# The delta stage's written order: masks ahead of the key scaling, value copies ahead of the exponentials, decayed products behind the state updates

## The chip, the cores and the metric

The kernel runs on one core of one Trainium2 chip. The metric is the device time of one execution in microseconds (us), the median of several runs. Five engines work side by side, each through its own queue in order: PE (TensorE, the matmuls, with its weight loads listed apart as PEld), DVE (VectorE), ACT (ScalarE), POOL (GpSimd) and SP (SyncE, which issues most of the DMAs here). An engine whose next instruction waits on a semaphore holds everything that stands behind it.

## What is computed

Two layers of a bidirectional hybrid encoder over 2048 tokens of width 1024. Each layer normalises its input, projects it, and runs two branches: a gated delta rule with four heads, scanned forward and backward in chunks, and a convolution module. Both are projected, merged with sigmoid gates, projected once more and added to the input. The stage that matters here is the chunked delta rule (the kernel uses chunks of 128 tokens):

```python
lmat = jnp.where(strict, jnp.einsum('bhncd,bhnsd->bhncs', k_beta, k) * decay, 0.0)
sol = lax.linalg.triangular_solve(eye + lmat, rhs, left_side=True, lower=True, unit_diagonal=True)
attn = jnp.einsum('bhncd,bhnsd->bhncs', q, k) * decay
...
def step(state, inp):
    val_n, kc_n, a_n, qd_n, kd_n, dl_n = inp
    v_new = val_n - jnp.einsum('bhcd,bhde->bhce', kc_n, state)
    o_n = jnp.einsum('bhcd,bhde->bhce', qd_n, state) + jnp.einsum('bhcs,bhse->bhce', a_n, v_new)
    state = state * dl_n[..., None, None] + jnp.einsum('bhcd,bhce->bhde', kd_n, v_new)
    return state, o_n
```

Each step needs the state of the step before: this is a chain that no reordering shortens. `decay` is the exponential of differences of cumulated log decays, masked to one triangle; it does not depend on the state, so it can be prepared ahead.

## The kernel before

Each layer runs a projection stage (dense matmuls, convolutions, per-head preparation), then `delta()`, then `merge()`. A dense matmul of float32 values is made of three passes (L173 to L175) over split operands: weights `whi`/`wlo` and inputs `hi`/`lo`. `weight()` (L159) loads a block by DMA into `wraw`, then ACT copies `whi` and DVE subtracts to give `wlo`.

`delta()` (L816) runs 16 steps; at each one the forward direction takes chunk `step` and the backward direction chunk `15 - step` (two lanes). Three kinds of work are written into one another:

- **The scan**, `lane()` (L956), in three parts. Part A: PE multiplies keys and queries with the state (L968, L971), DVE updates the values (L973), ACT copies the query part scaled into `o1` (L977), and in steps 8 to 15, where the other direction's output of this chunk is already stored, POOL adds it (`old`, L979). Part B: PE applies the inverse (L983), ACT copies the new values `vn` out of PSUM (L985). Part C: PE forms the state update and the output (L992, L1001), DVE updates the state (L995) and adds the output (L1003 or L1008).
- **The preparation** of later steps, `prep()` (L866): loads (`gb` from `gc_d`, `k` and `g` from `g_d`, inverse blocks); masks on POOL (L889) and exponentials on ACT (L892) of `gb`; transposes, copies (L896 to L904) and the products with the decay (L906, L908) on DVE; then four groups of small matmuls that assemble the inverse `wt` (L915; L925 and L928 with the copies L930 to L934; L939 and L940 with L942; L948 and L949 with L950 and L951). It is a generator; `go(i)` runs the next part for step `i`. The ring of `gb` has two buffers, one preparation's worth, so the `gc_d` loads of the next preparation wait for L908 of this one.
- **`finish()`** (L1014) of a step's two outputs from step 8 on: squares, the reciprocal root of their means, scaling, transposes, store.

`decay_keys` (L854) scales the next step's keys on POOL. Between these parts `pull(n)` takes `n` steps of dense work from a filler, one step being three matmul passes of 512 columns. The filler runs the second half of the gate projection, `gates(1)`: 16 column blocks times 2 times 8, or 256 steps. Then `early_merge()` (L1124, called from `filler()`, L1118) loads `u` by four DMAs, splits it in four pieces, and gives 64 more steps. A `yield GAP` ends a pull at once, without dense work: one stands behind the four loads of `u`, one behind each split.

`bind()` (L87) fixes the order of PE, ACT, DVE and POOL inside `delta()` to the order in which the program writes it. SP is not fixed: a planner orders its DMAs by its own estimate of when they are ready. `LEAD` gives the pulls before step 0, `STEP` the four pulls of a step, 17 dense steps in all.

The order of one step before: part A, inverse part 1 of step+1, key scaling, masks and exponentials of step+2, reciprocal root, pull 5; part B, output scaling, products of step+2, inverse part 2 of step+1, pull 4; part C, inverse part 3, loads of step+3, squares, pull 4; transposes, inverse part 4, pull 4.

Of the kernel before, what the change touches and what calls it, by code (L numbers as in the profile page):

```python
# [10 lines left out]
ALU = mybir.AluOpType  # L11
# [14 lines left out]
R1 = 3.0  # L26
R3 = 4.5
GAP = 0
LEAD = (16, 6, 8, 6, 4)
STEP = (5, 4, 4, 4)  # L30
TAIL = (3, 3, 3)
Z = '121'
# [24 lines left out]
def sort(ps):  # L57
    return ps.rearrange("p (i a) -> p a i", a=2)


def cut(x):
    return x.rearrange("p (a i) -> p a i", a=2)
# [13 lines left out]
class Trunk:  # L76
# [66 lines left out]
    def load(self, out, in_):  # L143
        self.nc.sync.dma_start(out, in_)
# [10 lines left out]
    def split(self, hi, lo, src):  # L155
        self.nc.scalar.activation(hi, src, AF.Copy)  # L156
        self.nc.vector.tensor_tensor(out=lo, in0=src, in1=hi.bitcast(F32), op=ALU.subtract)  # L157
# [658 lines left out]
    def delta(self):  # L816
        nc = self.nc
# [25 lines left out]
        def fetch(step):  # L843
            out = []
            for d in range(2):
                c = step if d == 0 else NCH - 1 - step
                kq = rkq().rearrange("p (h a c) -> p h a c", h=4, a=2)
                kv = rkv().rearrange("p (a h c) -> p a h c", h=4, a=2)
                self.load(kq, self.kq_d[c])
                self.load(kv, self.kv_d[c])  # L850
                out.append((c, kq, kv))
            return out

        def decay_keys(ins, d):  # L854
            c, _, kv = ins
            k2 = col(self.kf, d, c)
            nc.gpsimd.tensor_tensor(out=kv[:, 0], in0=kv[:, 0], in1=k2[:, :, None].to_broadcast([P, 4, P]),
                                    op=ALU.mult)
# [7 lines left out]
        def prep(step):  # L866
            ins, ks, gbs = [], [], []
# [3 lines left out]
            chunk = (step, NCH - 1 - step)  # L871
            for d, c in enumerate(chunk):
                g, k, gb = hv(rgq()), hv(rgk()), hv(rgb())
# [12 lines left out]
            for d, c in enumerate(chunk):  # L886
                gb = gbs[d]
                msk = self.con[:, C_MF if d == 0 else C_MB, :]
                nc.gpsimd.tensor_tensor(out=gb, in0=gb, in1=msk[:, None, :].to_broadcast([P, 4, P]), op=ALU.add)  # L889
                ng = col(self.ngc, d, c)  # L890
                for hd in range(H):
                    nc.scalar.activation(gb[:, hd, :], gb[:, hd, :], AF.Exp, bias=ng[:, hd:hd + 1])  # L892
# [7 lines left out]
            for b in range(4):  # L900
                r = blk(b)
                v_.tensor_copy(wt[r, :, 32 * b:32 * b + 32], dtm[r])
                d, q = (0, 32 * b) if b < 2 else (1, 32 * (b - 2))
# [52 lines left out]
        def lane(step, d, g, wt, c, kq, kv):  # L956
            s = hv(st_all[d])
            x = kv[:, 1]
            neg, dl, eg = col(self.neg, d, c), col(self.dl, d, c), col(self.eg, d, c)
            od = self.o_d[c].rearrange("p h e -> p (h e)")  # L960
            o1 = old = None
            if step >= NCH // 2:
                old = ro()
                self.load(old, od)
            if step:
                pk = hv(self.pz())
                for hd in range(H):
                    mm(pk[:, hd, :], kq[:, hd, 0, :], s[:, hd, :], start=True, stop=True)  # L968
                pq = hv(self.pz())
                for hd in range(H):  # L970
                    mm(pq[:, hd, :], kq[:, hd, 1, :], s[:, hd, :], start=True, stop=True)  # L971
                for hd in range(H):
                    v_.scalar_tensor_tensor(out=x[:, hd], in0=pk[:, hd, :], scalar=neg[:, hd:hd + 1], in1=x[:, hd],  # L973
                                            op0=ALU.mult, op1=ALU.add)
                o1 = ro1()
                for hd in range(H):
                    nc.scalar.activation(hv(o1)[:, hd, :], pq[:, hd, :], AF.Copy, scale=eg[:, hd:hd + 1])  # L977
                if old is not None:
                    nc.gpsimd.tensor_tensor(out=old, in0=old, in1=o1, op=ALU.add)  # L979
            yield  # L980
            pw = self.pz()
            for hd in range(H):
                mm(hv(pw)[:, hd, :], wt[:, 4 * d + hd, :], x[:, hd], start=True, stop=True)  # L983
            vn = rvn()
            nc.scalar.activation(vn, pw, AF.Copy)  # L985
            vn = hv(vn)
            yield

            if step < NCH - 1:
                pn = self.pz()  # L990
                for hd in range(H):
                    mm(hv(pn)[:, hd, :], kv[:, 0, hd], vn[:, hd, :], start=True, stop=True)  # L992
                if step:
                    for hd in range(H):
                        v_.scalar_tensor_tensor(out=s[:, hd, :], in0=s[:, hd, :], scalar=dl[:, hd:hd + 1],  # L995
                                                in1=hv(pn)[:, hd, :], op0=ALU.mult, op1=ALU.add)
                else:
                    nc.scalar.activation(st_all[d], pn, AF.Copy)
            po = self.pz()
            for hd in range(H):  # L1000
                mm(hv(po)[:, hd, :], g[:, hd, :], vn[:, hd, :], start=True, stop=True)  # L1001
            if old is not None:
                v_.tensor_tensor(out=old, in0=po, in1=old, op=ALU.add)  # L1003
                done.append((c, hv(old)))
                return
            o = ro()
            if step:
                v_.tensor_tensor(out=o, in0=po, in1=o1, op=ALU.add)  # L1008
                self.store(od, o)
            else:  # L1010
                nc.scalar.activation(o, po, AF.Copy)
                self.store(od, o)
# [40 lines left out]
        def pull(n):  # L1053
            for _ in range(n):
                if next(fill, GAP) == GAP:
                    return

        start = self.mark()
        nil = iter(())
        preps = [prep(i) for i in range(NCH)] + [nil, nil, nil]  # L1060
        go = lambda i: next(preps[i], None)
        go(0)
        ins = fetch(0)
        go(0)
        go(0)
        go(1)
        pull(LEAD[0])
        go(1)
        go(1)
        for d in range(2):  # L1070
            decay_keys(ins[d], d)
        for n in LEAD[1:4]:
            go(0)
            pull(n)
        go(2)
        ready = go(0)
        pull(LEAD[4])
        last = finish([])
        for step in range(NCH):
            nxt = fetch(step + 1) if step + 1 < NCH else None  # L1080
            gs, wt = ready
            lanes = [lane(step, d, gs[d], wt, *ins[d]) for d in range(2)]
            for x in lanes:
                next(x)
            go(step + 1)
            if nxt:
                for d in range(2):
                    decay_keys(nxt[d], d)
            go(step + 2)
            next(last)  # L1090
            pull(STEP[0])
            for x in lanes:
                next(x)
            next(last)
            go(step + 2)
            go(step + 1)
            pull(STEP[1])
            for x in lanes:
                next(x, None)
            go(step + 1)  # L1100
            go(step + 3)
            new = finish(list(done))
            done.clear()
            next(new)
            pull(STEP[2])
            next(last)
            ready = go(step + 1)
            last = new
            pull(STEP[3])
            ins = nxt  # L1110
# [13 lines left out]
    def early_merge(self):  # L1124
        nc = self.nc
        self.t1 = self.big([P, KD, HALF], F32, "t1")
        self.u0, load, split = self.operand_parts(self.u_d, 0, "uop")
        for k in range(4):
            load(k)
        yield GAP  # L1130
        ahead = self.weight(self.a["w_cf"][self.l, 0], 4)
        for k in range(4):
            split(k)
            yield GAP
        for j in range(KD):
            wc = ahead
            if j + 1 < KD:
                ahead = self.weight(self.a["w_cf"][self.l, j + 1], 4)
            for b in range(2):
                sl = slice(b * NB, (b + 1) * NB)  # L1140
                ps = self.pd()
                for more in self.dense_steps(ps, wc, lambda k: (self.u0[:, k, sl], self.u0[:, 4 + k, sl]), 4):
                    if more:
                        yield 1
                nc.scalar.activation(cut(self.t1[:, j, sl]), sort(ps), AF.Copy)
                yield 1
# [199 lines left out]
```

## Time and profile before

| | us |
|---|---|
| median of 3 runs | 3320.24 (3318.83 to 3320.41) |
| the profiled execution | 3318.64 |
| span of its trace | 3316.8 |
| PE busy | 3129.0 (94%) |
| PE weight loads busy | 2725.5 (82%) |
| DVE busy | 2397.4 (72%) |
| ACT busy | 1400.9 (42%) |
| POOL busy | 299.4 (9%) |

The first layer's delta stage lies between about 889 and 1340 us of the span, the second's between about 2510 and 2960 us. PE is the busiest engine, so the profile is read by what PE waits for. The rows of waits give, for an instruction, what released it, the total, the number of times and the longest. The rows of stretches give for each stretch its length, each engine's busy time with its count of instructions, the granted TensorE clock (1.00 is full speed), the DMA share and GB/s. The rows of the timeline give start, duration, engine, line, operation and tiles, with the idle time before and its releaser in brackets.

### The profile page before, as it was taken

To read this page: it belongs to the slowest core of one execution; us is meant where nothing else is said; L and a number is where in the kernel's file an instruction comes from. 1 tells how busy PE (TensorE), PEld (TensorE's weight loads), DVE (VectorE), ACT (ScalarE), POOL (GpSimd) and SP (SyncE) were. 2 spreads that over 40 slices of the span, in tenths; PEclk is the share of its full clock that TensorE was granted. 3 is DMA by queue.
4 is the path that set the end of the run, shared out by engine and by line. 5 is a ranking of instruction groups with operands and counts; after the bars stand their busy time and mean duration, and the time that the engine had idled before them with its cause. 6 is when DMAs were issued, how large, how long until landed. Compare 5 with 4: busy or idle time off the path is not lost. (4 is left out here: it accounts for less than half of the span.)

```text
span 3316.8 us, 50988 instructions
## 1 busy us (share of the span) xinstructions
PE 3129.0 (94%) x19110; PEld 2725.5 (82%) x19110; DVE 2397.4 (72%) x4401; ACT 1400.9 (42%) x3104; POOL 299.4 (9%) x297
## 2 busy tenths in 40 slices
PE   6999999999899997999999999999998999798998
PEld 5888888888788887787888888888887888687786
DVE  7698989896455586655676989898863556757655
ACT  5625252523354455533345343343234535555332
POOL 3000000000112221000000000000001212200000
PEclk9999999999999998999999999999999999899999
DMA  4323131335677675564413232223457777746634
GB/s 139 94 87 109 64 109 64 115 113 161 226 250 229 216 231 182 168 203 132 135 55 101 74 107 88 93 82 98 152 192 237 238 222 221 245 137 206 204 124 149
DMA packets 425878, 501.67 MB, mean 151 GB/s; under 512 B 95584, under 2 KB 260064, under 8 KB 425632
## 3 DMA queue, kind: packets, MB, share of 16 engines
q1 hardware_dynamic: 352880, 388.58, 38.1%
q10 hardware_dynamic: 64688, 80.09, 6.9%
q0 software_dynamic: 8064, 29.76, 2.4%
q8 instruction: 150, 2.46, 0.3%
q14 instruction: 96, 0.79, 0.1%
HBM read 342.74 MB, written 155.58 MB: 150 GB/s over the span
## 5 line engine op out<-in xcount | busy, mean ns | idle before, releaser
L173 PE MATMUL pd<-hhi,whi 128*128 128x512 f32 x2816 | 1096.4, 390 | 0.0
L175 PE MATMUL pd<-hhi,wlo 128*128 128x512 f32 x2816 | 1075.1, 382 | 18.6 <-DVE wlo L157 18.6
L174 PE MATMUL pd<-hlo,whi 128*128 128x512 f32 x2816 | 1075.5, 382 | 0.0
L734 DVE SCALAR_TENSOR_TENSOR cacc<-gp,vec,cacc 128x1009 f32<-128x1009 f32 (+1 forms) x480 | 616.9, 1285 | 38.3 <-ACT cacc L732 35.1
L175 PEld LDWEIGHTS pd<-hhi,wlo 128*128 128x128 f32 x2816 | 536.6, 191 | 97.7 <-DVE wlo L157 21.0
L173 PEld LDWEIGHTS pd<-hhi,whi 128*128 128x128 f32 x2816 | 536.9, 191 | 80.3 <-issue 1.4
L174 PEld LDWEIGHTS pd<-hlo,whi 128*128 128x128 f32 x2816 | 537.3, 191 | 73.8 <-issue 1.9
L156 ACT ACTIVATE whi<-wraw 128x512 fp32r<-128x512 f32 x400 | 242.5, 623 | 483.2 <-PE pd L174 312.2
L157 DVE TENSOR_TENSOR wlo<-wraw,whi 128x512 fp32r<-128x512 f32 x400 | 276.4, 706 | 217.4 <-ACT whi L156 216.7
L559 DVE SCALAR_TENSOR_TENSOR acc<-cin,vec,acc 128x1022 f32<-128x1022 f32 (+1 forms) x192 | 246.9, 1301 | 14.4 <-ACT acc L557 13.4
L175 PE MATMUL pd<-yhi,wlo 128*128 128x512 f32 x512 | 195.2, 381 | 4.8 <-DVE wlo L157 4.6
L173 PE MATMUL pd<-yhi,whi 128*128 128x512 f32 x512 | 195.0, 381 | 4.3 <-ACT whi L156 4.3
L174 PE MATMUL pd<-ylo,whi 128*128 128x512 f32 x512 | 194.0, 379 | 0.0
L812 ACT ACTIVATE go<-pd,vec 128x512 f32<-128x512 f32 x128 | 86.9, 679 | 144.0 <-PE pd L175 121.8
L535 ACT ACTIVATE cin<-pd 128x512 f32<-128x512 f32 x96 | 57.0, 594 | 156.8 <-PE pd L175 156.6
L1192 ACT ACTIVATE gt<-gt 128x1024 f32<-128x1024 f32 x64 | 67.6, 1057 | 114.9 <-DMA gt<-gt 100.8
L175 PEld LDWEIGHTS pd<-yhi,wlo 128*128 128x128 f32 x512 | 96.7, 189 | 22.0 <-DVE wlo L157 8.5
L973 DVE SCALAR_TENSOR_TENSOR dl<-pz,neg,dl 128x128 f32<-128x128 f32 x240 | 66.8, 345 | 66.2 <-PE pz L968 65.9
L892 ACT ACTIVATE dm<-dm,ngc 128x128 f32<-128x128 f32 x256 | 80.2, 391 | 81.1 <-POOL dm L889 80.8
L173 PEld LDWEIGHTS pd<-yhi,whi 128*128 128x128 f32 x512 | 96.8, 189 | 20.3 <-ACT whi L156 7.1
L173 PE MATMUL pd<-uop,whi 128*128 128x512 f32 x256 | 100.2, 391 | 11.9 <-ACT uop L156 6.4
L746 ACT ACTIVATE ao<-pd 128x512 f32<-128x512 f32 x64 | 38.3, 598 | 170.0 <-PE pd L175 169.9
(290 smaller groups left out, 4885.3 us busy)
## 6 DMA issues: line engine op xcount, KB each, us to landing
wraw<-w_in SPq DMA_DIRECT2D x240, 256.0 KB, 3.1
gt<-go ACTq DMA_DIRECT2D x128, 256.0 KB, 2.9
dl<-gr SPq DMA_DIRECT2D x128, 256.0 KB, 6.0
dl<-kq SPq DMA_DIRECT2D x64, 512.0 KB, 5.3
dl<-kv SPq DMA_DIRECT2D x64, 512.0 KB, 6.4
gt<-gt SPq DMA_DIRECT2D x64, 512.0 KB, 4.9
wraw<-w_out SPq DMA_DIRECT2D x96, 256.0 KB, 3.0
kq<-acc SPq DMA_DIRECT2D x16, 1024.0 KB, 5.6
```

Of the source, the lines that this page charges most:

```text
L156: self.nc.scalar.activation(hi, src, AF.Copy)
L157: self.nc.vector.tensor_tensor(out=lo, in0=src, in1=hi.bitcast(F32), op=ALU.subtract)
L173: mm(ps, whi[:, k, :], xhi, start=k == 0, stop=False)
L174: mm(ps, whi[:, k, :], xlo, start=False, stop=False)
L175: mm(ps, wlo[:, k, :], xhi, start=False, stop=k == kk - 1)
L535: nc.scalar.activation(cut(t[:, o + b * NB:o + (b + 1) * NB]), sort(ps), AF.Copy)
L559: self.nc.vector.scalar_tensor_tensor(out=out, in0=t[:, k:k + n], scalar=wc(k), in1=out, op0=ALU.mult, op1=ALU.add)
L734: self.nc.vector.scalar_tensor_tensor(out=acc, in0=t[:, k:k + n], scalar=wc(k), in1=acc, op0=ALU.mult, op1=ALU.add)
L812: nc.scalar.activation(cut(o), sort(ps), AF.Identity, bias=self.vec[:, V_GB + j:V_GB + j + 1])
L892: nc.scalar.activation(gb[:, hd, :], gb[:, hd, :], AF.Exp, bias=ng[:, hd:hd + 1])
L973: v_.scalar_tensor_tensor(out=x[:, hd], in0=pk[:, hd, :], scalar=neg[:, hd:hd + 1], in1=x[:, hd], op0=ALU.mult, op1=ALU.add)
L1192: nc.scalar.activation(gt, gt, AF.Sigmoid)
```

## The change

The masks of `prep()` become a part of their own (one `yield` more), and so does the addition of `old` in `lane()`. The order of a step becomes: part A without the addition of `old`, inverse part 1 of step+1, masks of step+2, addition of `old`, key scaling, reciprocal root, pull 5; part B, exponentials of step+2, output scaling, inverse part 2 of step+1, pull 4; part C, inverse part 3, products of step+2, loads of step+3, squares, pull 4; transposes, inverse part 4, pull 4. The lead before step 0 is rewritten: the same 40 dense steps, of which 8 now stand ahead of the first masks, exponentials and products. In `early_merge()` four GAPs instead of one stand behind the loads of `u`.

```diff
-LEAD = (16, 6, 8, 6, 4)
+LEAD = (8, 10, 6, 6, 6, 4)
...
                 nc.gpsimd.tensor_tensor(out=gb, in0=gb, in1=msk[:, None, :].to_broadcast([P, 4, P]), op=ALU.add)
+            yield
+            for d, c in enumerate(chunk):
+                gb = gbs[d]
                 ng = col(self.ngc, d, c)
                 for hd in range(H):
                     nc.scalar.activation(gb[:, hd, :], gb[:, hd, :], AF.Exp, bias=ng[:, hd:hd + 1])
...
                     nc.scalar.activation(hv(o1)[:, hd, :], pq[:, hd, :], AF.Copy, scale=eg[:, hd:hd + 1])
-                if old is not None:
-                    nc.gpsimd.tensor_tensor(out=old, in0=old, in1=o1, op=ALU.add)
+            yield
+            if old is not None:
+                nc.gpsimd.tensor_tensor(out=old, in0=old, in1=o1, op=ALU.add)
             yield
...
         ins = fetch(0)
+        pull(LEAD[0])
+        go(0)
         go(0)
         go(0)
         go(1)
-        pull(LEAD[0])
-        go(1)
+        pull(LEAD[1])
+        go(0)
         go(1)
         for d in range(2):
             decay_keys(ins[d], d)
-        for n in LEAD[1:4]:
-            go(0)
-            pull(n)
+        pull(LEAD[2])
+        go(1)
+        go(0)
+        pull(LEAD[3])
+        go(1)
+        go(0)
         go(2)
+        pull(LEAD[4])
         ready = go(0)
-        pull(LEAD[4])
+        pull(LEAD[5])
...
             go(step + 1)
+            go(step + 2)
+            for x in lanes:
+                next(x)
             if nxt:
                 for d in range(2):
                     decay_keys(nxt[d], d)
-            go(step + 2)
             next(last)
             pull(STEP[0])
             for x in lanes:
                 next(x)
+            go(step + 2)
             next(last)
-            go(step + 2)
             go(step + 1)
             pull(STEP[1])
             for x in lanes:
                 next(x, None)
             go(step + 1)
+            go(step + 2)
             go(step + 3)
...
         for k in range(4):
             load(k)
-        yield GAP
+        for _ in range(4):
+            yield GAP
```

## The prediction, made before the result was known

> **What bounds the kernel now.** I read the page's head first, then the stretches of the delta stage, then what PE waits for in them, then the timeline around those waits.
>
> ```profile
> span 3316.8 us, 50988 instructions
> ```
>
> ```profile
> 1000.00:1245.00 245.00, 229.03 (x2365) 203.95 (x2364) 162.29 (x423) 118.60 (x371) 56.80 (x49) 0.98 0.71 224
> 1245.00:1300.00 55.00, 36.83 (x353) 32.94 (x352) 35.03 (x90) 25.81 (x84) 10.59 (x10) 0.78 0.65 208
> 892.41:902.65 10.24, 4.98 (x12) 3.95 (x13) 3.94 (x7) 0.00 (x0) 0.31 (x1) 0.50 1.01 342
> 1083.55:1086.97 3.42, 1.41 (x13) 1.24 (x13) 3.32 (x9) 0.00 (x0) 0.00 (x0) 1.00 0.32 108
> 1086.97:1090.38 3.41, 3.41 (x25) 2.79 (x24) 3.36 (x12) 0.39 (x1) 0.00 (x0) 0.50 0.84 258
> ```
>
> In the steady scan (first row) PE is busy 229.03 of 245 us; in the 55 us after it only 36.83. So PE bounds the stage, and the change can take out only PE's idle time and what that idle time does to the clock. PE's waits in the first layer: before step 0 (870 to 1000), in the scan (1000 to 1245), where the gate work ends (1245 to 1300).
>
> ```profile
> PE pd L175 <- DVE wlo L157: 8.2, 1, 8.2
> PE pz L925 <- ACT dh L918: 2.3, 2, 1.9
> ```
>
> ```profile
> PE pz L1001 <- DVE dh L931: 8.5, 6, 2.0
> PE pz L992 <- ACT dm L985: 5.7, 3, 3.5
> PE pz L992 <- DVE dh L931: 1.8, 2, 0.9
> ```
>
> ```profile
> PE pz L992 <- ACT dm L985: 7.9, 1, 7.9
> PE pz L983 <- ACT dm L977: 5.2, 1, 5.2
> PE pd L173 <- ACT uop L156: 3.2, 1, 3.2
> ```
>
> The second layer, 2500 to 2920, shows the same in one list:
>
> ```profile
> PE pz L992 <- ACT dm L985: 14.0, 5, 8.1
> PE pd L175 <- DVE wlo L157: 7.9, 1, 7.9
> PE pz L1001 <- DVE dh L931: 7.5, 7, 1.8
> PE pz L983 <- ACT dm L977: 4.9, 1, 4.9
> PE pd L173 <- ACT uop L156: 3.2, 1, 3.2
> PE pz L925 <- ACT dh L918: 2.7, 2, 1.9
> PE pz L992 <- DVE dh L931: 2.4, 2, 1.5
> ```
>
> These rows add to 42.8 and 42.6 us. Why they arise is seen in step 4 (its first matmul is the row of PE), one fence per engine:
>
> ```profile
> 1020.20 1.05 PE L968 MATMUL pz<-dh,dl 128*128 128x128 f32 x8
> ...
> 1044.85 1.05 PE L968 MATMUL pz<-dh,dl 128*128 128x128 f32 x8
> ```
>
> ```profile
> 1025.34 2.51 POOL L889 TENSOR_TENSOR dm<-dm,con 128x512 f32<-128x512 f32 x2
> ```
>
> ```profile
> 1026.65 2.51 ACT L892 ACTIVATE dm<-dm,ngc 128x128 f32<-128x128 f32 x8 [1.37 <-POOL dm L889]
> ...
> 1031.20 1.06 ACT L985 ACTIVATE dm<-pz 128x512 f32<-128x512 f32 x2
> ```
>
> ```profile
> 1032.01 0.50 DVE L896 STREAM_TRANSPOSE dh<-dh 128x128 f32<-128x128 f32 x2
> 1032.55 1.18 DVE L902 COPY dl<-dh 32x256 f32<-32x256 f32 x4
> 1033.76 1.29 DVE L906 TENSOR_TENSOR dl<-dl,dm 128x512 f32<-128x512 f32 x2
> 1034.97 1.29 DVE L908 TENSOR_TENSOR dl<-dl,dm 128x512 f32<-128x512 f32 x2
> ```
>
> POOL masks behind the key scaling; ACT's exponentials wait for the masks and hold the value copies (L985); DVE's 4.3 us of products (0.50 + 1.18 + 1.29 + 1.29) stand ahead of the inverse copies (L930 to L934), and their PSUM buffer is what PE's output matmuls (L1001) then lack. All this is work for step+2, standing ahead of work for this step.
>
> **The change, part by part.** No compute instruction is added or removed, and PE's order in a step stays. What counts is what stands ahead of what.
>
> *Lead.* The 8.2 us are PE at the first gate steps, waiting for `wlo`:
>
> ```profile
> 888.85 2.87 POOL L839 MEMSET dl<- 128x1024 f32 x3 [8.48 <-PE pd L174]
> ```
>
> ```profile
> 896.93 1.29 DVE L157 TENSOR_TENSOR wlo<-wraw,whi 128x512 fp32r<-128x512 f32 x2
> ```
>
> The memsets can start only when the last gate work of the first half frees their memory (888.85); the products of step 0 need them, and `wlo` stood behind the products until 896.93. After, the first pull with its four `wlo` stands ahead of the products, so the wait goes; the memset and products lie beside 18 dense steps. The loads of step 1's preparation move behind the first pull's weights, on SP too, but nothing needs them before those 18 steps are over. The zn copy (L918) no longer stands behind exponentials either. Late next: the exponentials of step 0, now behind the first pull on ACT. Bounds for what is left: 0 and the old 10.5; I take 1.5 a layer, the nearest row being the 1.9 of L918. Gain (8.2 + 2.3 - 1.5) + (7.9 + 2.7 - 1.5), some **18 us**.
>
> *Scan.* I count from the step's first matmul at 1020.20 as 0; 24.65 us later the next begins, of which some 1.4 were stall, so 23. Masks lose the key scaling and the addition of `old` ahead of them. Their input must land first:
>
> ```profile
> dm<-gc SPq DMA_DIRECT2D x32, 256.0 KB, 4.1
> ```
>
> That load waits for L908 of the step before, because of the two buffers. The products now stand behind the state updates and output additions, which end about 17.4 by the PE order; so by my working they end at 21.7 instead of 16.1 (1034.97 + 1.29 less 1020.20). The load then lands about 3 in the next step, masks end at 5.5 to 6, and the exponentials, now behind the value copies (about 10), do not wait. Their slack is 4 us. SP's own queue behind this load (keys, values, inverse blocks of later steps) starts up to 6 us later; these have about a step's time to spare, since the planner fetches them a step ahead. On ACT the exponentials now hold the output scaling (needed for the transposes at about 19) and the inverse's L904; both would end by 15 to 19. On DVE the products now hold the next value updates:
>
> ```profile
> 1021.29 1.13 DVE L973 SCALAR_TENSOR_TENSOR dl<-pz,neg,dl 128x128 f32<-128x128 f32 x4 [2.81 <-PE pz L968]
> ```
>
> After 21.7 come the transposed outputs and inverse copies, so these updates start at about 25 (2 in the new step) instead of 1; PE needs them only after pull 5, at about 7. So both old waits go, and the cover of the new place is some 5 us; without it each us late would cost PE one us. Bounds: 0 left, or all of 16.0 and 15.8 left (7.5 + 2.4 + 14.0 less the 8.1 of the next part). I take 2 a layer, one wait of the size of the 2.0 above. Gain **28 us**.
>
> *Hand-over.* The gate work is 256 steps: 40 lead, 12 steps of 17, and 12 of step 12. There the filler turns to `u`. Before, five pulls in a row then give no dense work; after, eight (the rest of step 12, all of step 13, two of step 14). The pieces move three pulls later:
>
> ```profile
> 1257.18 1.06 ACT L156 ACTIVATE uop<-uop 128x1024 fp32r<-128x1024 f32 x1 [3.26 <-DMA uop<-u]
> ...
> 1268.30 2.50 ACT L892 ACTIVATE dm<-dm,ngc 128x128 f32<-128x128 f32 x8 [7.82 <-POOL dm L889]
> ```
>
> The first row is the cause of the 5.2 (the split waits for its load and holds `o1` and, over DVE, the value updates); it goes. The second is the cause of the 7.9 (exponentials ahead of the value copies); it goes as well, and so do the 3.2. But thirteen dense steps leave as cover. I worked the chain through with these durations: in step 13 PE waits about 1.3 for inverse copies and 2 for output scaling behind late exponentials; in step 14 about 6.5 for the value updates, which stand behind 4.3 of products, splits, weights and transposed outputs with only 5 us of PE work beside them; then 3.5 behind the reciprocal root and a split. That is 13.3 a layer against 16.3 and 16.2. Bounds: 5 (the split chain hidden but for step 14) to 27 (eight pulls at the old 16.3 / 5). Gain some **6 us**. The thirteen steps come back at the end of the stage, dense.
>
> *Clock.* After the 2.0 us stall near 1085 PE was busy 1.41 of 3.42 us, and the next 3.41 us were granted 0.50 with PE busy throughout: 1.7 us lost. In the 10.24 us at 0.50 after the lead's stall, busy 4.98, it was 2.5. In the scan the clock is 0.98: 4.9 us a layer. [...] I take 2.5 a layer in the lead, 4 in the scan, 1 in the hand-over (there the chain, not the clock, sets the pace): **15 us**.
>
> Sum: 18 + 28 + 6 + 15 = 67. The profiled execution took 3318.64, 1.8 above its span; 3318.6 - 67 = 3251.6, and the median of the runs lies 1.6 above that execution: **3253**.
>
> **The rivals.**
> *The empty pulls cost more* (0.15). Each pull without dense work costs what it did, 16.3 / 5 = 3.3: 8 times that is 26 a layer, 13 more than I took. For it: the chain of step 13 to 14 is long; against: three of the old waits had causes that go. 3253 + 26 = 3279.
> *The scan's waits only move* (0.14): PE waits for the value updates behind the products, or for the transposes, as long as it did for L985 and L931; scan and its clock (28 + 8) fall out. For it: DVE has 162.29 of 245 us to do; against: 5 us of cover. 3253 + 36 = 3289.
> *Slower* (0.08): the loop of `gc` load, masks, exponentials, products closes on itself. The products free the buffer for the load that the next products need; now both ends stand late in the step, and DVE holds the value updates behind them. It decides from the point where masks end about 14 us late (4 of slack ahead of the exponentials, 5 between these and the products, 5 of DVE cover), for instance because SP has the load behind others. Then each us more costs one in each of 14 steps a layer; at 3 us, 84, with the scan's gain gone: 3289 + 84 = 3373. Against it: load, masks, exponentials and products are 4.1 + 2.5 + 2.5 + 4.3, 13.4 of 23 us.
> *Short stalls cost no clock* (0.10 of the 0.59 below): if the dips in the scan have another cause than stalls of 2 us and less, they stay, and the scan's 8 us of clock fall out: 3253 + 8 = 3261, inside the forecast's own range. Against it: the two stretches at 1083.55 and 1086.97. [...]
> *No change* (0.04): the first two together and more, 3253 + 26 + 36 = 3315.
> That the written order isn't kept is no rival for four engines, since `bind` fixes it; only SP is free, as above.
>
> **How the numbers follow.** My forecast, 0.59, is 3253 with its own range 3225 to 3275: nearly no new stall, or twice what I kept. The first two rivals lie at 3279 and 3289; the range for 8 in 10 is 3222 to 3298. Below it lies only the case that nothing at all is left. About 0.2% (6.6 us) is what a measurement of this kernel can tell from no change. Faster by more: 0.59 + 0.15 + 0.14 = 0.88; within: 0.04; slower: 0.08.
>
> **What would show it.** Lead: no wait of L175 for `wlo` near 889, else that step is wrong. Scan: no rows L1001 or L992 behind L931 and L985; a row of L983 behind L973 or L977 in steps 1 to 12 speaks for the second rival. ACT's idle time ahead of L892 should shrink towards zero; if it grows, the loop of the slower rival is at work. Hand-over: waits of L983 and L968 in steps 13 and 14, in sum 13 a layer; above 20 is the first rival. Clock: 1.00 in the steady scan. The forecast is wrong if PE's idle time in the stage falls by less than 35 us in sum.

## The result and the profile after

| | before | after |
|---|---|---|
| median (lowest to highest), us | 3319.69 (3318.83 to 3320.41), 4 runs | 3245.24 (3243.90 to 3250.80), 4 runs |
| ratio, 95% interval | 1 | 0.9779 (0.9762 to 0.9796) |
| span of the profiled execution, us | 3316.8 | 3242.1 |

The kernel became 74.5 us faster; 3253 was forecast, with a range of 3222 to 3298. Where the 74.7 us of the span went is seen by cutting each layer's delta stage at three instructions that both kernels have: the first state matmul (L968 before, L971 after) of step 1, that of step 13, and the first matmul on `gop` in `merge()`. The lead's stretch begins at one and the same gate matmul. Stretches of the kernel before (columns as before: length, busy time of PE, PEld, DVE, ACT and POOL, granted clock, DMA share, GB/s), lead, scan and hand-over of layer 1, then of layer 2:

```profile
878.30:949.70 71.40, 61.27 (x493) 51.89 (x492) 27.93 (x55) 25.05 (x55) 14.48 (x13) 0.93 0.81 262
949.70:1250.60 300.90, 283.57 (x2936) 252.92 (x2934) 196.87 (x516) 145.39 (x442) 65.93 (x57) 0.98 0.72 229
1250.60:1354.80 104.20, 85.63 (x673) 75.94 (x672) 60.18 (x158) 58.42 (x169) 14.53 (x12) 0.89 0.56 173
2510.40:2571.10 60.70, 50.86 (x445) 42.81 (x444) 26.83 (x54) 22.63 (x51) 13.89 (x12) 0.92 0.86 277
2571.10:2870.80 299.70, 283.84 (x2935) 253.06 (x2933) 196.29 (x516) 145.50 (x442) 66.06 (x57) 0.98 0.73 230
2870.80:2974.70 103.90, 83.92 (x676) 74.08 (x673) 59.10 (x158) 59.05 (x170) 14.07 (x12) 0.90 0.55 170
```

The same stretches of the kernel after:

```profile
880.50:947.70 67.20, 60.94 (x493) 51.98 (x492) 25.82 (x56) 28.36 (x67) 13.24 (x12) 0.95 0.82 266
947.70:1224.10 276.40, 275.10 (x2935) 248.82 (x2933) 192.68 (x513) 146.67 (x443) 68.78 (x58) 1.00 0.78 251
1224.10:1321.90 97.80, 83.59 (x676) 75.05 (x673) 64.98 (x164) 61.76 (x172) 14.08 (x12) 0.91 0.60 192
2473.10:2528.40 55.30, 50.30 (x445) 42.75 (x444) 25.09 (x54) 25.99 (x63) 12.96 (x11) 0.94 0.87 284
2528.40:2803.90 275.50, 274.95 (x2935) 248.86 (x2933) 189.69 (x513) 146.61 (x443) 69.71 (x58) 1.00 0.79 252
2803.90:2901.60 97.70, 83.59 (x675) 74.98 (x672) 65.35 (x164) 61.65 (x172) 14.06 (x12) 0.91 0.59 189
```

PE's counts show that the same matmuls lie in each pair. Length less PE's busy time is PE's idle time; the rest of a difference is matmuls that ran faster.

| both layers, us | gained | of it PE's idle time | of it PE's busy time | forecast, with its clock |
|---|---|---|---|---|
| lead | 9.6 | 8.7 | 0.9 | 23 |
| scan | 48.7 | 31.3 | 17.4 | 36 |
| hand-over | 12.6 | 10.2 | 2.4 | 8 |

The other 3.8 us of the 74.7 lie outside the stage. The scan is saturated: 1.30 and 0.55 us of idle time are left in some 276 us a layer, at clock 1.00. That the sum lies as near as it does is in part luck: the lead brought 13.4 us less than forecast and the scan 12.7 us more.

What PE waits for after, in the first layer's lead, and then in its hand-over:

```profile
PE pz L928 <- ACT dh L921: 6.3, 1, 6.3
```

```profile
PE pz L971 <- DVE dm L1050: 10.4, 2, 6.0
PE pz L1005 <- DVE dh L934: 3.8, 2, 1.9
```

**The lead** lost the 8.2 us behind `wlo` and got 6.3 us of another wait. Timeline of ACT and of SP's queue around it, kernel after:

```profile
912.01 1.38 ACT L156 ACTIVATE whi<-wraw 128x512 fp32r<-128x512 f32 x2 [8.84 <-DMA wraw<-w_in]
913.30 0.26 ACT L921 ACTIVATE dh<-pz 128x128 f32<-128x128 f32 x1
```

```profile
903.94 2.44 SPq L144 DMA_DIRECT2D dm<-gc  x2
906.43 0.91 SPq L144 DMA_DIRECT2D wraw<-w_in  x2
```

The weight load of the third column block is issued at 906.43, behind loads of step 1's preparation that were moved into this place: the `gc` loads need the buffers of step 0's products (`gb` has two), which end at 903.24, and so could go only at 903.94. On ACT the conversion of those weights waits 8.84 us, and behind it stands the inverse's copy L921, a quarter of a microsecond long, for which PE waits. So one load that is issued late, in SP's queue, holds up ACT's queue and with it PE.

**The hand-over** has about as much waiting left as was forecast (14.2 a layer against 13.3), but behind another instruction. DVE of the kernel after, in step 13:

```profile
1243.39 1.28 DVE L911 TENSOR_TENSOR dl<-dl,dm 128x512 f32<-128x512 f32 x2
...
1246.62 1.22 DVE L157 TENSOR_TENSOR uop<-uop 128x1024 fp32r<-128x1024 f32 x1 [0.25 <-ACT uop L156]
1247.77 0.74 DVE L1050 SCALAR_TENSOR_TENSOR dm<-pz,vec,dm 128x512 f32<-128x512 f32 x1
```

The state matmuls L971 lack a PSUM buffer that L1050 (transposed outputs) frees, the 10.4 us above, and L1050 stands behind the products (L911) and a split of `u`.

### The profile page after: what moved, and what is told of

It is laid out like the page before. It is cut to its first block, busy times and chain, and to the rows that moved or that the text cites. A ratio compares the mean times of both kernels' runs of the same rounds, so it can differ in the third digit from the quotient of the medians.

```text
span 3242.1 us, 51095 instructions
## 1 busy us (share of the span) xinstructions
PE 3110.2 (96%) x19110; PEld 2719.2 (84%) x19110; DVE 2392.3 (74%) x4401; ACT 1397.2 (43%) x3100; POOL 303.1 (9%) x297
## 5 line engine op out<-in xcount | busy, mean ns | idle before, releaser
L157 DVE TENSOR_TENSOR wlo<-wraw,whi 128x512 fp32r<-128x512 f32 x400 | 290.0, 738 | 217.6 <-ACT whi L156 207.9
L559 DVE SCALAR_TENSOR_TENSOR acc<-cin,vec,acc 128x1022 f32<-128x1022 f32 (+1 forms) x192 | 246.5, 1298 | 14.6 <-ACT acc L557 13.4
L889 POOL TENSOR_TENSOR dm<-dm,con 128x512 f32<-128x512 f32 x64 | 82.1, 1299 | 534.8 <-DMA dm<-gc 494.4
L174 PEld LDWEIGHTS pd<-ylo,whi 128*128 128x128 f32 x512 | 96.8, 189 | 15.7 <-DVE ylo L157 2.3
L980 ACT ACTIVATE dm<-pz,eg 128x128 f32<-128x128 f32 x240 | 68.5, 368 | 95.8 <-PE pz L974 89.8
```

Source lines behind the costliest of these rows:

```text
L174: mm(ps, whi[:, k, :], xlo, start=False, stop=False)
L559: self.nc.vector.scalar_tensor_tensor(out=out, in0=t[:, k:k + n], scalar=wc(k), in1=out, op0=ALU.mult, op1=ALU.add)
```

## The experiments

Each kernel is an edit of the kernel after, and the diffs run from that. The table gives the ratio to the kernel before on the same chip (it took 3318 to 3324 us on these chips, so rows are better compared by ratio than by median), and for layer 1 and layer 2 the lengths (us) of the stretches defined above. M, X and P say which of the scan's three moves stand: **m**asks in front of the old addition and key scaling, e**x**ponentials behind the value copies, **p**roducts behind the state updates.

| run | moves, GAPs | median | ratio (95%) | lead | scan | hand-over |
|---|---|---|---|---|---|---|
| before | none, 1 | 3319.69 | 1 | 71.4 / 60.7 | 300.9 / 299.7 | 104.2 / 103.8 |
| after | M X P, 4 | 3245.24 | 0.9779 (0.9762 to 0.9796) | 67.2 / 55.3 | 276.4 / 275.5 | 97.7 / 97.7 |
| e1_old_lead | M X P, 4 | 3259.68 | 0.9807 (0.9792 to 0.9821) | 71.1 / 60.8 | 276.8 / 276.1 | 99.3 / 97.2 |
| e7_old_scan | none, 4 | 3316.73 | 0.9977 (0.9966 to 0.9987) | 66.6 / 55.7 | 300.6 / 299.7 | 107.6 / 108.2 |
| e10_old_scan_one_gap | none, 1 | 3315.38 | 0.9985 (0.9974 to 0.9995) | 66.5 / 55.5 | 298.7 / 301.0 | 104.2 / 105.6 |
| e11_masks_only | M, 4 | 3250.06 | 0.9789 (0.9773 to 0.9806) | 65.8 / 55.6 | 279.3 / 279.4 | 97.3 / 97.0 |
| e12_exps_only | X, 4 | 3296.25 | 0.9927 (0.9913 to 0.9942) | 66.3 / 55.5 | 290.4 / 289.7 | 108.9 / 107.7 |
| e6_masks_late_exps_early | P, 4 | 3282.94 | 0.9902 (0.9885 to 0.9919) | 66.9 / 55.2 | 287.9 / 285.0 | 110.8 / 110.0 |
| e3_products_back | M X, 4 | 3251.23 | 0.9782 (0.9767 to 0.9797) | 66.9 / 55.8 | 280.6 / 280.2 | 97.5 / 97.1 |
| e4_exps_early | M P, 4 | 3241.30 | 0.9769 (0.9756 to 0.9782) | 67.4 / 56.1 | 275.1 / 274.9 | 98.9 / 98.1 |
| e5_masks_late | X P, 4 | 3263.86 | 0.9836 (0.9820 to 0.9852) | 66.6 / 55.7 | 277.3 / 276.6 | 107.1 / 103.5 |
| e2_one_gap | M X P, 1 | 3244.07 | 0.9764 (0.9750 to 0.9779) | 66.2 / 55.5 | 276.4 / 276.2 | 95.9 / 93.7 |
| e8_inverse_first | M X P, 4 | 3234.86 | 0.9743 (0.9726 to 0.9760) | 65.0 / 54.1 | 276.9 / 276.1 | 98.4 / 97.4 |
| e14_first_one_gap | M X P, 1 | 3232.99 | 0.9730 (0.9717 to 0.9744) | 63.2 / 55.1 | 276.5 / 276.6 | 93.5 / 95.4 |

### Lead and scan apart

The kernel after with the old lead (e1_old_lead):

```diff
-LEAD = (8, 10, 6, 6, 6, 4)
+LEAD = (16, 6, 8, 6, 4)
...
         ins = fetch(0)
-        pull(LEAD[0])
         go(0)
         go(0)
         go(0)
         go(1)
-        pull(LEAD[1])
-        go(0)
+        pull(LEAD[0])
         go(1)
-        for d in range(2):
-            decay_keys(ins[d], d)
-        pull(LEAD[2])
         go(1)
-        go(0)
-        pull(LEAD[3])
         go(1)
-        go(0)
+        for d in range(2):
+            decay_keys(ins[d], d)
+        for n in LEAD[1:4]:
+            go(0)
+            pull(n)
         go(2)
-        pull(LEAD[4])
         ready = go(0)
-        pull(LEAD[5])
+        pull(LEAD[4])
```

> Only the lead is that of before. Theory (the lead is worth no more than the 2 to 4 us a layer by which the starts of step 1 differ in the two traces, because PE's wait for wlo was followed by a new wait of 6.3 and 5.0 us for L921): 3251, with the 8 us wait of L175 for wlo back and the wait of L928 for L921 gone or at 2. Rival (the prediction's working: the lead is worth its old waits and their clock, 23 us): 3268.

3259.68, between the two theories. The ratios differ by 0.0028 of 3320 us, 9 us; their intervals just overlap, but the stretches of the lead say the same (71.1 and 60.8 against 67.2 and 55.3). So the new lead is worth some 9 us, well under half of the 23 forecast.

The kernel after with the step's order of before, that is new lead and four GAPs alone (e7_old_scan):

```diff
-            go(step + 1)
-            go(step + 2)
             for x in lanes:
                 next(x)
+            go(step + 1)
             if nxt:
                 for d in range(2):
                     decay_keys(nxt[d], d)
+            go(step + 2)
+            go(step + 2)
             next(last)
             pull(STEP[0])
             for x in lanes:
                 next(x)
-            go(step + 2)
             next(last)
+            go(step + 2)
             go(step + 1)
             pull(STEP[1])
             for x in lanes:
                 next(x, None)
             go(step + 1)
-            go(step + 2)
             go(step + 3)
```

> The new lead and the four GAPs stay, the order of the 16 steps is that of before. Theory (the scan's order brings 24 us in each layer between the start of step 1 and of step 13, as the two traces differ there): 3245 + 49, and some 8 more where the gate work ends, because the exponentials stand ahead of the value copies again, so 3295 to 3305, and L1005 behind the inverse copies and L996 behind the value copies are back as PE's waits. Rival (the lead and the GAPs carry most, the scan's waits only move): 3275 or less.

Both missed: the scan is as long as before (300.6, 299.7), and the hand-over, now with four GAPs, is some 4 us longer a layer (3.4 and 4.4), which gives most of the lead's 4.8 and 5.0 back. The ratio's interval leaves 4 to 11 us of gain. So the same with one GAP (e10_old_scan_one_gap):

> The scan's order as before and the single empty pull as before, with the new lead alone. The run of the old order with four empty pulls took 3316.7 beside 3324.0 of the kernel before. Theory, that the three more empty pulls are worth nothing with the new order but cost some with the old one (there the exponentials stand in front of value copies that then have no dense work as cover): 3306 to 3313 where the kernel before has 3320 to 3324, that is the new lead's 9 to 14 us alone. Rival, that the new lead is worth nothing without the new scan: 3315 to 3322.

3315.38 beside 3318.24 of the kernel before: the number is in the rival's range, but the ratio's interval says 2 to 9 us faster, and the stretches of the lead are as much shorter as in the kernel after (4.9 and 5.2). What the GAPs do is taken up below. In all, the scan's order carries nearly the whole gain: between e7_old_scan and the kernel after lie 0.0198 of 3320, 66 us.

### Which of the scan's three moves

One move put back at a time. Products back in front of the inverse copies (e3_products_back):

```diff
             next(last)
+            go(step + 2)
             go(step + 1)
             pull(STEP[1])
             for x in lanes:
                 next(x, None)
             go(step + 1)
-            go(step + 2)
             go(step + 3)
```

> Only the products go back in front of the inverse copies; masks stay first and exponentials behind the value copies. Theory (the place on DVE decides): the products must now wait for exponentials that end at about 12.6 us of the step, so the inverse copies end near 18 where PE needs them at 13.5: about 3.5 us a step in 28 steps, 3245 + 70 to 100, slower than the kernel before, all of it as waits of L1005 or L996 behind L934. Rival (only the waits behind the inverse copies that the trace of before had come back, 8 us a layer and their clock): 3262 to 3270.

Neither came: the ratio is 0.9782, with that of the kernel after within the interval. The scan is some 4 us a layer longer (280.6, 280.2), with 3.2 us of waits for L934 in layer 1. Exponentials back in front of the value copies (e4_exps_early):

```diff
                     decay_keys(nxt[d], d)
+            go(step + 2)
             next(last)
             pull(STEP[0])
             for x in lanes:
                 next(x)
-            go(step + 2)
             next(last)
```

> The changed kernel with one thing put back: the exponentials stand in front of the scan's value copies again (masks still in front of key scaling, products still late). Theory, that the scan's 24 us a layer come from the exponentials no longer standing in front of the value copies on ACT: each of some 12 steps a layer gets back a stall of 1 to 2.5 us (the exponentials take 2.5) with the matmuls that need the value copies waiting for them, 3270 to 3300 us, the granted clock in the scan under 1.00. Rival, that the early masks alone do it, since with them the exponentials are over before the values arrive (masks ended near 1025.8, the value copies began at 1027.15, 2.4 us of exponentials between): under 3258.

This is the rival's number, 0.9769. Beside the other two, the scan needs the exponentials' move no more than the products'. Masks back behind the key scaling (e5_masks_late):

```diff
             go(step + 1)
-            go(step + 2)
             for x in lanes:
                 next(x)
             if nxt:
                 for d in range(2):
                     decay_keys(nxt[d], d)
+            go(step + 2)
             next(last)
```

> The changed kernel with one thing put back: the masks stand behind the addition of the old output and the key scaling again; exponentials still behind the value copies, products still late. Theory (the exponentials' place carries the gain): 3242 to 3255, since the masks then end some 3 us later and the exponentials, behind the value copies, wait a little for them while PE waits for neither. Rival (the early masks carry it): 3270 to 3300, with idle time of ACT behind the masks and waits of PE behind the inverse's and output's ACT work.

The time lies between the two, 19 us above the kernel after. The scan is as good (277.3, 276.6), as the theory said; the hand-over is 9 and 6 us longer, and there the rival's waits came (shown below). Any two of the three moves thus remove all or nearly all of the scan's stalls. Then each alone. Products alone (e6_masks_late_exps_early, the last two edits together):

> The changed kernel with masks behind the key scaling and exponentials in front of the value copies, as before; of the scan's edits only the late products stay. Both theories of the two runs beside this one: the waits for the value copies are back, 3285 to 3305 (the scan's gain gone, the late products keeping a part: the waits for the inverse copies behind the products, 8.5 and 7.5 us before, stay away). If it lies under 3260 neither masks nor exponentials matter and the products' place does, against the earlier run with the products put back.

Masks alone (e11_masks_only), and exponentials alone (e12_exps_only), the other two put back as in the diffs above:

> The changed kernel with only the first of the scan's three moves left: masks in front of the old output's addition and the key scaling; the exponentials back in front of the value copies and the products back in front of the inverse copies; new lead and four empty pulls. So far, of the three moves any two gave a scan without a wait in it (the runs with products, exponentials or masks put back), and the late products alone gave half. Theory, that the early masks alone do it, because exponentials and products then run in idle time before values and inverse arrive: no more than 5 us of waits in the scan of a layer, 3240 to 3255 us. Rival, that at least two moves are needed: the 2 us stalls behind exponentials or products are back, 3270 to 3300.

> The changed kernel with only the second of the scan's moves left: the exponentials behind the value copies; masks behind the key scaling and products in front of the inverse copies as before; new lead and four empty pulls. Theory, that with late masks this only trades one wait for the other: no waits for the value copies, but the exponentials end some 3 us later than before (near the inverse copies) and the products behind them hold the inverse copies for 2 to 5 us a step, 3290 to 3340. Rival (any one of the moves gives about half, as the late products alone did): 3275 to 3290.

Products alone took 3282.94, just under the forecast range, with 13.0 and 14.7 of the scan's 24.5 and 24.2 us. Masks alone held to their theory: 3250.06. For the exponentials 3296.25 lies in the theory's range, with 10.5 and 10.0 us of the scan, and the waits are those it named, though rarer and shorter (in layer 1 seven, of at most 2.5 us, and not 2 to 5 us in every step). What PE waits for from step 1 to 13 of layer 1 sorts all four. No move (e10_old_scan_one_gap), masks alone, exponentials alone, products alone:

```profile
PE pz L1005 <- DVE dh L934: 7.6, 6, 2.2
PE pz L996 <- ACT dm L989: 5.9, 5, 2.6
PE pz L996 <- DVE dh L934: 2.4, 2, 1.5
```

```profile
PE pz L996 <- ACT dm L989: 0.9, 1, 0.9
PE pz L1005 <- DVE dh L934: 0.8, 1, 0.8
...
```

```profile
PE pz L1005 <- DVE dh L934: 10.4, 7, 2.5
```

```profile
PE pz L996 <- ACT dm L989: 8.4, 5, 2.5
```

The exponentials' move removes the waits for the value copies (L989) and leaves those for the inverse copies (L934); the products' move does it the other way round; the masks' move removes nearly all of both. Layer 2 says the same. Why one can do it is in the kernel before. POOL in step 4:

```profile
1024.34 1.04 POOL L857 TENSOR_TENSOR dl<-dl,kf 128x512 f32<-128x512 f32 x1 [5.37 <-DMA dl<-kv]
```

The key scaling waited 5.37 us for its load, and the masks stood behind it until 1025.34, with no wait of their own: by the trace their `gc` loads had landed by 1012.62. ACT's exponentials then idled 1.37 us for them (quoted in the prediction), and behind the exponentials stood, on ACT, the weight conversion and the value copies; `wlo` on DVE follows that conversion, the products follow `wlo`, the inverse copies follow the products. One load at the head of POOL's queue made three queues late.

That is the smaller part. Of the 17.3 us of PE's idle time in layer 1's scan, 11.6 lie in steps 8 to 12, and there the other instruction ahead of the masks holds them, the addition of `old`. POOL and ACT of the kernel before in step 9, whose first matmul starts at 1147.91:

```profile
1151.24 1.27 POOL L979 TENSOR_TENSOR dm<-dm,dm 128x512 f32<-128x512 f32 x1 [19.24 <-ACT dm L977]
...
1156.13 2.50 POOL L889 TENSOR_TENSOR dm<-dm,con 128x512 f32<-128x512 f32 x2
```

```profile
1157.43 2.51 ACT L892 ACTIVATE dm<-dm,ngc 128x128 f32<-128x128 f32 x8 [4.43 <-POOL dm L889]
```

The addition waits for `o1`, which ACT makes from this step's own state matmuls; so the masks start 8.2 us into the step, though their loads had landed by 1147.12, and ACT idles 4.43 us for them.

With masks alone, PE, POOL, ACT and DVE in step 4, whose first matmul starts at 1014.20:

```profile
1021.59 1.95 PE L987 MATMUL pz<-dl,dl 128*128 128x128 f32 x16
```

```profile
1017.89 1.04 POOL L857 TENSOR_TENSOR dl<-dl,kf 128x512 f32<-128x512 f32 x1 [6.22 <-DMA dl<-kv]
```

```profile
1019.14 2.45 ACT L895 ACTIVATE dm<-dm,ngc 128x128 f32<-128x128 f32 x8
...
1023.63 1.07 ACT L989 ACTIVATE dm<-pz 128x512 f32<-128x512 f32 x2
```

```profile
1027.40 1.29 DVE L911 TENSOR_TENSOR dl<-dl,dm 128x512 f32<-128x512 f32 x2
1028.72 0.28 DVE L933 COPY dh<-pz 32x128 f32<-32x128 f32 x1
```

The key scaling waits 6.22 us for the same load, and the exponentials no longer hang on it, as the masks have run before. The exponentials have no wait ahead of them and are over at 1021.59, when PE's matmuls for the new values (L987) only begin, though they still stand in front of the value copies. These start 9.4 us into the step, where in the kernel before it was 11.0. The products still stand in front of the inverse copies, which follow at 1028.72 at once, 14.5 us into the step instead of 16.1; 0.8 us is the longest wait that this causes in the scan. With masks early the products' move brings 4.2 and 4.5 us a layer more by the stretches (279.3 and 279.4 to 275.1 and 274.9); by the times the two kernels' intervals overlap. The exponentials' move brings nothing then.

### The masks in the hand-over

The four kernels with late masks and four GAPs are 6 to 13 us a layer longer there than the kernel after. Masks late (e5_masks_late), PE's longest wait, then POOL, then ACT:

```profile
PE pz L1049 <- ACT dm L1044: 10.9, 1, 10.9
```

```profile
1241.67 1.26 POOL L983 TENSOR_TENSOR dm<-dm,dm 128x512 f32<-128x512 f32 x1 [9.46 <-DMA dl<-kq]
...
1244.88 2.58 POOL L889 TENSOR_TENSOR dm<-dm,con 128x512 f32<-128x512 f32 x2
```

```profile
1246.22 2.55 ACT L895 ACTIVATE dm<-dm,ngc 128x128 f32<-128x128 f32 x8 [12.33 <-POOL dm L889]
```

The same thing happens on a larger scale: the masks stand behind the key scaling and the addition of `old`, POOL idles 9.46 us ahead of that addition, and ACT idles 12.33 us for the masks. Behind the exponentials stands the output scaling (L1044), for which PE's transposes (L1049) wait. The row of the addition names a load of keys, which the addition does not read; in the run with exponentials alone the row of the addition at 1249.94, with 7.86 us of idle time, names its own load, `dm<-o`. In the kernel after the masks ran ahead of that addition:

```profile
1230.40 2.49 POOL L889 TENSOR_TENSOR dm<-dm,con 128x512 f32<-128x512 f32 x2 [17.76 <-DMA dm<-gc]
1232.85 1.27 POOL L983 TENSOR_TENSOR dm<-dm,dm 128x512 f32<-128x512 f32 x1
```

### One empty pull or four

One GAP behind the loads of `u`, as before (e2_one_gap):

```diff
-        for _ in range(4):
-            yield GAP
+        yield GAP
```

> One GAP behind the loads of u in place of four. Theory (the three GAPs more pay for themselves, because a split that waits for its load holds ACT): PE waits some 5 us for the value updates in step 13 and 3 at the first u matmul, but thirteen more dense steps cover step 14; 3248 to 3255. Rival (empty pulls cost 3 us each, more than the wait for the load): 3230 to 3240.

The time, 3244.07, lies between the two ranges, and 0.9764 beside 0.9779 have overlapping intervals: the times don't decide it. The stretches point one way in all three pairs with one GAP and four: 95.9 and 93.7 against 97.7 and 97.7; 104.2 and 105.6 against 107.6 and 108.2 in the old order; 93.5 and 95.4 against 98.4 and 97.4 with the lead below. By these lengths the three more GAPs cost some 2 to 5 us a layer. They do remove what they were made for: with one GAP, layer 1 still has waits of 3.4 us behind L980 and 3.1 behind the split of `u`. But PE's idle time in the hand-over is 11.2 and 11.6 us with one GAP and 14.2 and 14.1 with four, so they cost more elsewhere than they save.

### The lead's new wait

Two dense steps fewer in the second pull, so that the first inverse copies L921 stand ahead of the third column block's weights (e8_inverse_first):

```diff
-LEAD = (8, 10, 6, 6, 6, 4)
+LEAD = (8, 8, 8, 6, 6, 4)
```

> The changed kernel with the second pull of the lead two steps shorter and the third two longer, so that the first inverse copies of step 0 stand on ACT in front of the third column block's weight conversion. Theory, that the wait of 6.3 and 5.0 us in the lead (and the half clock of 6.8 us behind it) comes from that conversion, which waits for a weight load issued late: the wait falls under 2 us a layer and the run lies 8 to 16 us under the changed kernel, 3230 to 3237 beside 3245 (ratio to the kernel before 0.973 to 0.976). Rival, that something else in the chain of the inverse is as late (the products, the transposes): no change, ratio 0.977 to 0.979.

The time is the theory's, 0.9743, but the wait went from 6.3 and 5.0 to 2.7 and 3.4 and not under 2. ACT and DVE with this lead:

```profile
902.53 0.28 ACT L921 ACTIVATE dh<-pz 128x128 f32<-128x128 f32 x1 [0.46 <-ACT go L812]
910.46 1.35 ACT L156 ACTIVATE whi<-wraw 128x512 fp32r<-128x512 f32 x2 [7.65 <-DMA wraw<-w_in]
```

```profile
911.12 2.58 DVE L157 TENSOR_TENSOR wlo<-wraw,whi 128x512 fp32r<-128x512 f32 x2 [8.98 <-ACT whi L156]
913.74 0.28 DVE L933 COPY dh<-pz 32x128 f32<-32x128 f32 x1
```

L921 is ahead of the late weights now; the inverse copies L933, on DVE, are still behind them. The wait shrank with the copies' place, so the late conversion is its cause; the load itself is as late as it was. The profiled execution of this run was 6.6 us over its median, so its stretches (3.4 us shorter in the two leads) and its time (0.0036 of 3320, 12 us) don't agree in size; that the lead is better both say, how much stays open.

Both edits together (e14_first_one_gap):

> The changed kernel with two things altered together: the lead of the run with the inverse first (pulls of 8, 8, 8, 6, 6, 4) and one empty pull in place of four. If both gains add (ratios to the kernel before of 0.9743 and 0.9764 beside 0.9779 of the changed kernel), 3222 to 3232 us, ratio 0.970 to 0.975. Rival, that the empty pulls are worth nothing and the 0.0015 between those two runs is chance: the run with the inverse first again, 0.974 to 0.977.

The ratio, 0.9730, is in the range of added gains (3232.99 is 1 us above that in us), but it is also within the interval of the lead alone: that the one GAP adds is not shown. By the ratios it is some 16 us under the kernel after, and 2.7% under the kernel before.

## Why the prediction was right, step by step

**Lead: the term was sized too large**, 18 us and 5 of clock against 9.6. The wait for `wlo` went, as said. The step that failed is "the loads of step 1's preparation move behind the first pull's weights, on SP too, but nothing needs them before those 18 steps are over". True, but what counts in a queue is who stands behind: the next block's weight load did. I kept 1.5 a layer after the row of 1.9 for L918; the same copy, L921 now, cost 6.3 and 5.0. The clock's part did not come either: 5.19 us of PE's work still ran at half clock, 2.6 us lost, where 2.5 were lost before. These are stretches of the kernel after, before and behind that wait:

```profile
905.14:911.97 6.83, 2.21 (x11) 1.59 (x9) 0.00 (x0) 0.00 (x0) 1.74 (x2) 1.00 1.06 310
911.97:918.80 6.83, 5.19 (x59) 4.22 (x60) 5.73 (x15) 5.68 (x16) 3.74 (x3) 0.50 0.88 251
```

**Scan: right in mechanism, too small in size**, 28 and 8 of clock against 48.7. The two old waits went and all but 1.3 and 0.55 us of idle time with them, so the 2 us a layer that I kept were not needed. PE's busy time for the same matmuls fell by 8.5 and 8.9 us where 4 of clock were taken. The clock itself was nearly right: the scan before has three stretches of 3.41 us at half clock in each layer, at most 5.1 us lost. The term that was missing is the other 3.4 and 3.8 us, whose cause stays open. Most positions came out as worked out: counted from the first state matmul of step 4 at 1018.06, the products end at 21.3 (21.7 was said), the value copies at 10.2 (about 10), the exponentials do not wait. But by the trace the `gc` loads landed at 4.4 and 6.3 instead of about 3, and the masks ended at 7.7 instead of 5.5 to 6, so of the 4 us of slack about 2.3 were there:

```profile
1018.06 1.05 PE L971 MATMUL pz<-dh,dl 128*128 128x128 f32 x8
```

```profile
1027.15 1.06 ACT L989 ACTIVATE dm<-pz 128x512 f32<-128x512 f32 x2
1028.10 2.44 ACT L895 ACTIVATE dm<-dm,ngc 128x128 f32<-128x128 f32 x8
```

```profile
1038.03 1.28 DVE L911 TENSOR_TENSOR dl<-dl,dm 128x512 f32<-128x512 f32 x2
```

What the prediction did not see is that the three moves are not a sum: it gave each wait a move of its own, and the runs show that the masks' move alone takes nearly all of both.

**Hand-over: the waits that are left have the size that was said, for another reason; the gain is half as large again (12.6 against 8).** 14.2 us of waits came where 13.3 were said, with the wait for L1050's buffer in place of "6.5 for the value updates". The stretch gained 6.4 and 6.2, because before it had 18.6 and 20.0 us of idle time where I counted 16.3 and 16.2. What the working did not price is the three more empty pulls by themselves: the runs show that early masks shorten the hand-over (by 6 to 13 us a layer) and that the three GAPs lengthen it, by 2 to 5.

**Clock.** 15 was said in sum; PE's busy time fell by 20.7, of it 17.4 in the scan, where the half-clock stretches account for some 10.

**The rivals.** That *the empty pulls cost more*, 26 us a layer in all, fell: 14.2 and 14.1 are left, and the three more cost 2 to 5. That *the scan's waits only move* fell: 1.3 and 0.55 us are left in it. *Slower* by the loop of load, masks, exponentials and products: the run with masks late and both others late has the whole loop at its latest, and its scan is within 1.1 us of the kernel after's, so the loop has room in a step of 23 us. *Short stalls cost no clock* fell: the scan's clock went from 0.98 to 1.00, and was 0.98 again where the old order brought stalls back, none of them over 2.6 us. That is the old scan with one GAP:

```profile
1000.00:1220.00 220.00, 206.93 (x2131) 183.84 (x2130) 141.57 (x377) 105.23 (x327) 46.17 (x40) 0.98 0.73 227
```

## What to carry to other kernels

Look for the first queue that holds work for nothing: a cheap instruction (2.5 us of masks) behind ones that wait, for a load or for this step's own results, made two more engines late, and moving it alone brought 21.6 and 20.3 of the 24.5 and 24.2 us a layer by which the reordering shortened the scan. Before a load or an instruction is moved, ask who stands behind it in its new place, not when its own result is needed. When several moves are made at once, test each alone and each taken away: here any two of three removed nearly all of the scan's stalls, so taking away one would have called each of them nearly worthless there.

## What the runs showed of the hardware

In the delta stages the traces of the two kernels show half clock in stretches of 3.41, 6.83 and 10.24 us, and once, in the second hand-over of the kernel before, of 17.06 us (2878.97 to 2896.03). In the scan of layer 1 of the kernel before, half clock followed three stretches in which PE was idle for about half or more: the pair in the prediction, the stretch ahead of 1134.76 (PE busy 0.09 of 3.41 us), and this one, with PE busy 1.73 us and no idle gap over 1.7 us:

```profile
1189.37:1192.79 3.42, 1.73 (x25) 1.48 (x24) 3.27 (x11) 1.65 (x5) 0.00 (x0) 1.00 0.46 86
1192.79:1196.20 3.41, 3.41 (x15) 2.64 (x11) 2.83 (x9) 0.90 (x4) 0.00 (x0) 0.50 0.89 279
```

In the same scan a stretch that was as idle was followed by full clock:

```profile
1162.06:1165.48 3.42, 1.72 (x15) 1.55 (x15) 3.33 (x8) 2.98 (x10) 0.00 (x0) 1.00 0.07 26
1165.48:1168.89 3.41, 3.41 (x33) 2.94 (x32) 3.35 (x12) 0.38 (x1) 0.00 (x0) 1.00 0.67 201
```

So with PE busy for about half of a stretch the scan shows both outcomes; after the less busy ones (0.09 and 1.41 us) came half clock. The three slow stretches cost at most 5.1 us, half of 3 times 3.41; PE's busy time fell by 8.5. The other 3.4 us are not explained.
